# Attention gates of the second macro tile: seven products of quarters in the common order instead of a plain product ahead of the other two groups

## The chip, the cores and the metric

The kernel runs on one core of one Trainium2 chip. The metric is the device time of one execution in microseconds (us); less is better. A core has TensorE (PE, with its weight loads shown as PEld), VectorE (DVE), ScalarE (ACT), GpSimd (POOL) and SyncE (SP), whose queue issues nearly all transfers here. Each engine works through its own instructions in the order in which they were written.

## The reference

One encoder layer over 4096 tokens of width 1024:

```
h = rmsnorm(x, pre_norm_g)
q, k, v, g_a, u_p, g_p = split(h @ w_in)
a = banded_attention(q, k, v, rel_bias, sink) * silu(g_a)   # 8 heads, 2 kv heads, |i-j| <= 128
p = multiscale_pool(u_p, pool_w, pool_scale) * silu(g_p)    # windows 2/4/8/16, mean minus token
x = x + rmsnorm(concat(a, p) @ w_out, post_norm_g)
```

The change touches g_a alone, and the order of the work around it: 512 columns of the input projection, called the attention gates, group QG below.

## The kernel before

The kernel has two halves. The first makes u_p (with pool_w folded into its weights), g_p and g_a, applies the pooling, and stores pooled rows and gates in DRAM (`yp_scr`, `ga_scr`). The second makes q, k and v, the attention and the output projection. The change is in the first half.

**Tiles.** The first half goes over eight macro tiles of 512 tokens, m = 0 to 7; "the second macro tile" is m = 1. The three groups of 512 output columns are QU (u_p), QP (the pool gates) and QG (the attention gates). Every float32 operand is carried as a pair of float16 tiles, a high part and a rest, and a product takes three matmuls: high x high, rest of the weights x high, high x rest of x. The high part is written by ACT (`x_hi`, `t_high`), the rest by DVE (`x_lo`, L303; `t_low`, L526), which reads the high part.

**Products of quarters.** From m = 1 on a group's block of 512 tokens by 512 columns is split in two along tokens, inputs and columns, and is done by seven products of quarters instead of eight (the scheme of Strassen and Winograd). One product (`product`, L990) is 4 x 3 x 2 = 24 matmuls of 128x256. `STEPS` gives the order: A11, A12, S2, S1, S4, S3, A22, where S1 to S4 are sums of quarters of x (`x_sum`, L310, on DVE). In the common order the three groups take turns within each step: QU, QP, QG. After a product ACT copies the PSUM bank (`keep`, L1002), or DVE joins it with a kept one (`join`, L1015); for the gates the SiLU follows on ACT (`gates`, L1024).

**Weights.** `wa` holds for each group seven blocks ("slots") of quarters. Macro tile 0 uses the plain quarters. For the seven products the sums of weight quarters must be formed: `t_sums` (L502, four DVE operations for a pair of column tiles), then `t_high` on ACT (L521) and `t_low` on DVE (L526) for four results of each pair. A group has two pairs: 4 and 5 for QG. Each pair fills one half of the columns of a slot, so a product needs both pairs. Results 3 and 2 go to slots 4 and 2, which the products S2 and S1 read (`t_last`); results 0 and 1 go to slots 5 and 6, for S3 and A22 (`t_first`). Slot 2 holds a plain quarter until then.

**The second macro tile before.** It begins with the attention gates as a plain product: `plain_ga` (L1051), four times 48 matmuls, straight from PSUM through the SiLU. The sums of the QG weights are formed while and after these run. Then QU and QP take their seven products by turns. From m = 2 on all three groups follow the common order.

**What sets the order.** Nothing is scheduled by a tool: `due(t, fn, ...)` notes a time for every step, the plan is sorted by these times, and each engine gets its instructions in that order. The times are only keys of the sort; an instruction runs when its engine reaches it and what it waits for is done. `t1` is the start of macro tile 1 (about 92.4 us in the profile), `PT` = 2.62 a product, `MACRO` = 21 `PT` a macro tile, `T0[m]` the start of tile m.

**Around it.** For macro tile m + 1, during tile m: `x_nat` loads x by rows (`xn`), `x_nat_square` squares them on ACT (L202), `x_scale` makes row scales on POOL, `rs_row` stores them (L268), `rs_spread` reads them back spread over all partitions (`rb`, L272), `y_load` loads x transposed (`ybig`, L282), `y_scale` multiplies (L292, DVE). `pooling(m, j)` is a chain on DVE (L855 to L883) for pooling group j of tile m. During tile 1 the kernel also prepares the weights of v (`wb_tile`; its norm is a small matmul on PE, L427, read by DVE, L133 to L149), and `out_scales` computes small scales on DVE.

Of the kernel before, what the change touches and what calls it, by code (L numbers as in the profile page):

```python
# [71 lines left out]
def hybrid_layer(ctx: ExitStack, tc, io, out):  # L72
# [82 lines left out]
    with ExitStack() as actx:  # L155
# [25 lines left out]
        def due(t, fn, *args):  # L181
            plan.append((t, len(plan), fn, args))
# [852 lines left out]
        def direct_gates(m, q):  # L1035
            silus(m, q, 1, 0, acc_t[m, q, "a"])

        ga_bank = {}

        def plain_ga(m, n, h):  # L1040
            ga_bank[n, h] = acc = (
                psa.tile([P, 2, HALF], F32, name=f"pg{n}{h}", tag="wup", bufs=3) if n
                else gemm.tile([P, 2, HALF], F32, name=f"pg{n}{h}", tag=f"acc{QG}")
            )
            i = 0
            for w in range(2):
                x = couple(m, "XW"[h])[:, w]
                for k in range(HK):
                    for wi, xi in ((0, 0), (1, 0), (0, 1)):
                        for c in range(2):  # L1050
                            nc.tensor.matmul(  # L1051
                                acc[:, c],
                                wa[:, QG, wi, (2 * n + w) * HK + k, c * P : (c + 1) * P],
                                x[:, xi, k, :], start=(i == 0), stop=(i > 3 * 2 * KT - 3),
                                skip_group_check=True,
                            )
                            i += 1

        def plain_gates(m, n, h):
            silus(m, QG, n, h, ga_bank[n, h])  # L1060

        def ga_store(m, n, h):
            s = s_t.pop((m, n, h))
            b0 = m * BPM + 2 * h
# [214 lines left out]
        t_last(5, t1 + 24.0)  # L1279


        def macro_x(m, t, op, s21, s4, s3, ys):

            cast(m, "S4", s4)
            cast(m, "S3", s3)
            if m > 1:
                cast(m, "S2", t + 8.7)
                cast(m, "S1", t + 9.7)
            if m + 1 == NM:
                return  # L1290
# [103 lines left out]

        for m in range(1, NM):
            t0 = T0[m]
            if m == 1:
                quads, z = (QU, QP), t0 + 21.0
            else:
                quads, z = (QU, QP, QG), t0  # L1400
            step = len(quads) * PT

            def op_at(i, z=z, step=step):
                return z + i * step

            if m == 1:
                macro_x(
                    1, t0, op_at, t0 + 15.0, op_at(2) + 0.3, op_at(2) + 1.5,
                    (t0 + 34.0, t0 + 35.2, t0 + 41.0, t0 + 43.6),
                )  # L1410
                x_ahead(3, t0 + 10.0)
            else:
                macro_x(
                    m, t0, op_at, t0 + 11.5, t0 + 17.2, t0 + 19.1,
                    (t0 + 21.0, t0 + 22.2, t0 + 28.5, t0 + 29.7),
                )
                x_ahead(m + 2, t0)
# [1106 lines left out]
```

## Time and profile before

| what | us |
|---|---|
| median of three runs | 1169.52 (1168.46 to 1170.8) |
| span of the profiled execution, first to last instruction | 1163.3 |
| PE busy | 1128.0 (97%) |
| DVE busy | 924.2 (79%) |
| ACT busy | 758.0 (65%) |
| POOL busy | 283.8 (24%) |

The page gives the profiled execution by its span, and no time of its own apart from the three runs; the span is 6.2 below their median, since it leaves out what lies before the first and behind the last instruction. The first half of the kernel reaches to about 490 us. Most of a busy engine's time costs nothing by itself; what counts is what PE waits for, since it is busy nearly all the time. In a timeline a row is a run of like instructions: its start, the time from the start of the first to the end of the last, engine, line, operation, tiles, shapes, how many, and in brackets how long the engine was idle ahead of it and what ended that. In windows a row is a stretch of time with each engine's busy time.

### The profile page before, as it was taken

The page shows a single profiled execution, that of the slowest core. Times are in us where ns is not written, and L with a number is a line of the kernel's source. Part 1 is how long each engine was busy: PE and PEld are TensorE (multiplying, and loading weights), DVE is VectorE, ACT ScalarE, POOL GpSimd, SP SyncE. Part 2 cuts the span into 40 slices and gives each one's busy share as a digit, 9 for nine tenths or more (in the row PEclk, how much of TensorE's full clock was granted, in tenths as well). Part 3 has the DMA queues.
Part 4 walks back from the last instruction along what each step waited for, and adds up shares of the span by engine and source line. Part 5 has one row for each costly group of instructions (what it writes and reads, how often), then busy time and mean ns, then how long its engine had stood idle before and what let it go on. Part 6 is the DMA issues. An engine that isn't in the chain of part 4 may idle for free.

```text
span 1163.3 us, 30484 instructions
## 1 busy us (share of the span) xinstructions
PE 1128.0 (97%) x12528; PEld 833.6 (72%) x12528; DVE 924.2 (79%) x1910; ACT 758.0 (65%) x1696; POOL 283.8 (24%) x270
## 2 busy tenths in 40 slices
PE   5999999999999999999999999999999999999997
PEld 4548888888888888887576676667666666766643
DVE  5788887778878886957887878878778778778896
ACT  5756666676465635166687767777677776777673
POOL 1000000000000000001454444454354444544322
PEclk9999999999999999999999999999999999999999
DMA  9577898696989856989799989899799899899877
GB/s 265 149 237 271 211 259 286 260 310 219 305 244 264 276 198 173 344 285 259 196 191 214 211 213 212 183 235 211 157 228 216 189 219 207 201 222 212 176 187 217
DMA packets 312635, 265.00 MB, mean 228 GB/s; under 512 B 214528, under 2 KB 275584, under 8 KB 303792
## 3 DMA queue, kind: packets, MB, share of 16 engines
q1 hardware_dynamic: 308464, 248.38, 78.1%
q0 software_dynamic: 4032, 14.68, 7.4%
q8 instruction: 98, 1.61, 0.5%
q14 instruction: 41, 0.34, 0.1%
HBM read 132.97 MB, written 79.21 MB: 182 GB/s over the span
## 4 chain that ended last, share of the span: by engine, by line
PE 45%; DVE 3%; DMA 3%; ACT 1%; issue 1%; SPq 0%; DVEq 0%; POOLq 0%; ACTq 0%
PE ms L2017 11%; PE aq_p L1754 9%; PE m L2017 8%; PE s L1532 4%; PE kv L1493 3%; PE kv L1716 3%; PE o L1870 3%; DMA pt_all<-pn 2%; PE z L1989 1%; PE o L1847 1%; DMA xt<-x_scr 1%; DVE pn L1605 1%; DVE p_all L1550 1%; PE ob L1847 1%; PE s L1989 0%
## 5 line engine op out<-in xcount | busy, mean ns | idle before, releaser
L990 PEld LDWEIGHTS <-wa 128*128 128x128 f16 x3360 | 329.7, 98 | 43.5 <-issue 4.8
L990 PE MATMUL ch<-xt,wa 128*128 128x256 f16 x1920 | 214.5, 274 | 2.6 <-ACT cbig L1002 1.7
L1561 ACT ACTIVATE p_all<-p_all,nm 128x384 f32<-128x384 f32 (+1 forms) x256 | 152.4, 596 | 41.3 <-DVE nm L1550 41.3
L1605 DVE SCALAR_TENSOR_TENSOR pn<-p_all,rd,pn 128x384 f16<-128x384 f32 (+1 forms) x256 | 144.5, 624 | 36.9 <-ACT pn L1597 36.1
L2017 PE MATMUL ms<-wo,ys 128*128 128x512 f16 x720 | 165.4, 379 | 2.9 <-DVE ys L1923 0.9
L1597 ACT ACTIVATE pn<-p_all,rd 128x384 f16<-128x384 f32 (+1 forms) x256 | 134.7, 597 | 36.6 <-DVE rd L1583 17.6
L1550 DVE CUSTOM_DVE_ANT_0 p_all<-s,ybig,nsink 128x384 f32<-128x384 f32 (+1 forms) x256 | 155.6, 663 | 1.7 <-PE s L1532 1.7
L2017 PEld LDWEIGHTS <-ys 128*128 128x128 f16 x720 | 68.8, 98 | 83.9 <-issue 2.5
L2017 PE MATMUL m<-wo,y 128*128 128x512 f16 x540 | 124.0, 379 | 1.4 <-DVE mo L2059 1.3
L990 PE MATMUL cl<-xt,wa 128*128 128x256 f16 x960 | 106.7, 273 | 0.8 <-DVE cbig L1015 0.6
L1923 POOL TENSOR_TENSOR y<-yf,y 128x512 f16<-128x512 f32 x29 | 33.5, 1157 | 270.4 <-DMA wo<-w_scr 158.9
L2017 PEld LDWEIGHTS <-y 128*128 128x128 f16 x540 | 51.6, 98 | 62.4 <-issue 2.5
L1754 PEld LDWEIGHTS <-raw 128*128 128x128 f16 x864 | 83.3, 98 | 18.0 <-issue 5.4
L211 POOL TENSOR_SCALAR ssq<-ssq 128x4 f32<-128x4 f32 (+1 forms) x11 | 3.6, 325 | 348.5 <-ACT jk L202 342.7
L1754 PE MATMUL aq_p<-xt,raw 128*128 128x256 f16 x672 | 77.9, 273 | 1.1 <-DVE nm L1550 1.1
L303 DVE TENSOR_TENSOR xt<-ybig,xt 128x1024 f16<-128x1024 f32 x56 | 67.2, 1219 | 13.0 <-ACT xt L298 11.4
L1923 POOL TENSOR_TENSOR ys<-at,ys 128x512 f16<-128x512 f32 x28 | 33.8, 1205 | 147.5 <-ACT ys L1919 123.9
L1532 PE MATMUL s<-k_all,q 64*32 64x288 f16 (+7 forms) x3432 | 63.1, 265 | 1.5 <-ACT k_all L1481 0.9
L1024 ACT ACTIVATE gp<-cbig,cg 128x256 f32<-128x256 f32 x42 | 19.0, 499 | 67.8 <-DVE cbig L1015 64.6
L2054 POOL TENSOR_TENSOR mo<-mo,ybig 128x512 f32<-128x512 f32 x39 | 51.4, 1317 | 44.2 <-ACT jkb L2043 43.9
L298 ACT CAST xt<-ybig 128x1024 f16<-128x1024 f32 x56 | 57.1, 1040 | 4.0 <-PE cl L990 2.1
L1754 PE MATMUL aq_p<-xt,wq_b 128*128 128x256 f16 x504 | 58.6, 273 | 0.0
(211 smaller groups left out, 1948.7 us busy)
## 6 DMA issues: line engine op xcount, KB each, us to landing
x_scr<-xt SPq DMA_DIRECT2D x16, 1024.0 KB
xt<-x_scr SPq DMA_DIRECT2D x16, 1024.0 KB
xn<-in_x SPq DMA_DIRECT2D x28, 512.0 KB
ybig<-in_xT SPq DMA_DIRECT2D x28, 512.0 KB
y_scr<-xt SPq DMA_DIRECT2D x14, 1024.0 KB
xt<-y_scr SPq DMA_DIRECT2D x14, 1024.0 KB
mo<-in_x POOLq DMA_DIRECT2D x28, 512.0 KB, 7.5
out<-mo SPq DMA_DIRECT2D x28, 512.0 KB
```

Of the source, the lines that this page charges most:

```text
L298: nc.scalar.copy(couple(m, c)[:, w, 0], y_view(i))
L303: eng.tensor_tensor(out=o[:, w, 1], in0=y_view(i), in1=o[:, w, 0], op=ALU.subtract)
L990: nc.tensor.matmul(acc[:, c], wa[:, q, wi, slot * HK + k, c * P : (c + 1) * P], x[:, xi, k, :], start=(fresh and n == 0), stop=(n > 3 * 2 ...
L1532: nc.tensor.matmul(s_bank[jj][r0 : r0 + nr, gg, c0:c1], q_t[u, half][a, qi, jj, tl + r0 : tl + r0 + nr], k_all[a, ki, kc : kc + c1 - c0], ...
L1550: nc.vector.tensor_tensor_reduce(out=p_t[b, half][:, hh, :nk], in0=s_t[b, half][jj][:, gg, :nk], in1=bias[:, h, lo : lo + nk], scale=negc[ ...
L1561: nc.scalar.activation(p[:, hh, :nk], p[:, hh, :nk], AF.Exp, bias=nm_t[b, half][:, hh : hh + 1], scale=-1.0, accum_out=den_t[b, half][:, h ...
L1597: nc.scalar.activation(prob_view(b, half)[:, 0, i], p_t[b, half][:, i, :nk], AF.Copy, scale=rd_t[b, half][:, 0, i : i + 1],)
L1605: nc.vector.scalar_tensor_tensor(out=pn4[:, 1, i], in0=p_t[b, half][:, i, :nk], scalar=rd_t[b, half][:, 0, i : i + 1], in1=pn4[:, 0, i], o ...
L1754: nc.tensor.matmul(acc[:, jj], w[:, wi, jj, k, :], x[:, xi, k, :], start=(first and n == 0), stop=(last and n > 3 * 2 * HK - 3), skip_grou ...
L1923: eng.tensor_tensor(out=y[:, :, 1], in0=f(u), in1=y[:, :, 0], op=ALU.subtract)
L2017: nc.tensor.matmul(z_t[u, tag], y[:, k, yi, :], wo[o][:, wi, k, :], start=(n == 0 and acc is None), stop=(n == 3 * HK - 1), skip_group_che ...
L2054: eng.tensor_tensor(out=mo, in0=mo, in1=gpost[:, cs], op=ALU.mult)
```

## The change

The plain product of the attention gates in tile 1 goes. QG takes its seven products in tile 1 by turns with QU and QP, as in the later tiles; tile 1 lasts 21 products, and the later tiles start 2.62 us earlier by the plan. The sums of the QG weights get new times (results 3 and 2 of each pair ahead, 0 and 1 later), and so do the loads of x for tile 2 and 3, the spread of the row scales of tile 2, and the y loads, scalings and casts in tile 1, which follow the later tiles' pattern.

```
-        def plain_ga(m, n, h):
...
-        def plain_gates(m, n, h):
-            silus(m, QG, n, h, ga_bank[n, h])
...
-        x_loads(2, (t1 - 20, t1 - 8), (t1 - 18, t1 + 4), (t1 - 6, t1 + 6), (t1 + 6, t1 + 13))
-        due(t1 + 27.0, rs_spread, 2)
-        for i, n, h in ((0, 0, 0), (1, 1, 0), (2, 0, 1), (3, 1, 1)):
-            due(t1 + 5.24 * i, plain_ga, 1, n, h)
-            due(t1 + 5.24 * i + 5.4, plain_gates, 1, n, h)
-            due(t1 + 5.24 * i + 6.9, ga_store, 1, n, h)
-        t_first(4, t1 + 14.3)
-        t_last(4, t1 + 18.5)
-        t_first(5, t1 + 19.5)
-        t_last(5, t1 + 24.0)
+        x_loads(2, (t1 - 20, t1 - 8), (t1 - 18, t1 - 6.7), (t1 - 6, t1 + 2), (t1 - 5, t1 + 3.3))
+        due(t1 + 14.0, rs_spread, 2)
+        due(t1 + 12.0, t_sums, 4)
+        t_last(4, t1 + 14.9)
+        due(t1 + 16.5, t_sums, 5)
+        t_last(5, t1 + 19.4)
+        for s1, d in ((4, 27.0), (5, 31.0)):
+            for i in (0, 1):
+                due(t1 + d + 1.2 * i, t_high, s1, i)
+                due(t1 + d + 0.75 + 1.2 * i, t_low, s1, i)
...
-        T0 = [0.0, t1] + [t1 + 21.0 + 14 * PT + MACRO * i for i in range(NM - 1)]
+        T0 = [0.0] + [t1 + MACRO * i for i in range(NM)]
...
-            if m == 1:
-                quads, z = (QU, QP), t0 + 21.0
-            else:
-                quads, z = (QU, QP, QG), t0
...
-            if m == 1:
-                macro_x(
-                    1, t0, op_at, t0 + 15.0, op_at(2) + 0.3, op_at(2) + 1.5,
-                    (t0 + 34.0, t0 + 35.2, t0 + 41.0, t0 + 43.6),
-                )
-                x_ahead(3, t0 + 10.0)
...
+            macro_x(
+                m, t0, op_at, t0 + (13.0 if m == 1 else 11.5), t0 + 17.2, t0 + 19.1,
+                (t0 + 21.0, t0 + 22.2, t0 + 28.5, t0 + 29.7),
+            )
+            x_ahead(m + 2, t0)
             for i in range(7):
-                for c, q in enumerate(quads):
+                for c, q in enumerate((QU, QP, QG)):
```

**DVE, early in tile 1.** The place is behind the rests of S2 and S1 of x. `L502` are the sums of weight quarters, `L526` rests of such sums (`wa`), `L1015` joins, `L855` to `L883` pooling, `L303` rests of x (`xt`). Before:

```order
L303 TENSOR_TENSOR xt<-ybig,xt 128x1024 x2
L502 TENSOR_TENSOR cbig<-cbig 128x512 x4
L526 SCALAR_TENSOR_TENSOR wa<-cbig,sc,wa 128x4x128 x3
L502 TENSOR_TENSOR cbig<-raw 128x512
L502 TENSOR_TENSOR cbig<-raw,cbig 128x512
L502 TENSOR_TENSOR raw<-raw 128x512
L502 TENSOR_TENSOR raw<-raw,cbig 128x512
L526 SCALAR_TENSOR_TENSOR wa<-cbig,sc,wa 128x4x128
L526 SCALAR_TENSOR_TENSOR wa<-raw,sc,wa 128x4x128 x2
L526 SCALAR_TENSOR_TENSOR wa<-cbig,sc,wa 128x4x128 x2
L1015 TENSOR_TENSOR u_0_1323<-pb_2_1266,cbig 128x2x256
```

Now, from the second rest of pair 4 (result 2) to the first of pair 5 (result 3), the last that the gates' product S2 needs; ahead of these rows stand the four sums of pair 4, the joins of QU, QP and QG after A12, the pooling of group 0, and pair 4's first rest:

```order
L526 SCALAR_TENSOR_TENSOR wa<-cbig,sc,wa 128x4x128
L502 TENSOR_TENSOR cbig<-raw 128x512
L502 TENSOR_TENSOR cbig<-raw,cbig 128x512
L502 TENSOR_TENSOR raw<-raw 128x512
L502 TENSOR_TENSOR raw<-raw,cbig 128x512
L855 TENSOR_TENSOR ws_1_0_1181<-u_0_632 128x527
L855 TENSOR_TENSOR ws_1_1_1183<-ws_1_0_1181 128x525
L862 TENSOR_TENSOR ws_1_1_1183<-ws_1_1_1183,edge 128x8
L875 SCALAR_TENSOR_TENSOR yt_1_1186<-ws_1_1_1183,u_0_632 128x512
L883 SCALAR_TENSOR_TENSOR yt_1_1186<-yt_1_1186,usc,gp_0_423 128x512
L303 TENSOR_TENSOR xt<-ybig,xt 128x1024
L526 SCALAR_TENSOR_TENSOR wa<-cbig,sc,wa 128x4x128
```

Before, all sums of weights stood ahead of the joins and the pooling; now joins, two pooling groups and the rest of S4 stand among them.

**DVE, late in tile 1.** `L149` ends the norm of v's weights, `L450` to `L701` are small scales, `u_1` is QU's join after S3. Before:

```order
L701 SCALAR_TENSOR_TENSOR rowsc<-rowsc,psc 128x4
L292 TENSOR_TENSOR ybig<-ybig,rb_1292 128x1024
L303 TENSOR_TENSOR xt<-ybig,xt 128x1024
L542 SCALAR_TENSOR_TENSOR raw<-raw,sc 128x1024
L303 TENSOR_TENSOR xt<-ybig,xt 128x1024
L1015 TENSOR_TENSOR u_1_1543<-cl_2_1551,cbig 128x2x256
L855 TENSOR_TENSOR ws_2_0_1608<-u_1_676 128x527
L855 TENSOR_TENSOR ws_2_1_1610<-ws_2_0_1608 128x525
L855 TENSOR_TENSOR ws_2_2_1612<-ws_2_1_1610 128x521
```

Now:

```order
L875 SCALAR_TENSOR_TENSOR yt_2_1493<-ws_2_2_1490,u_1_676 128x512
L883 SCALAR_TENSOR_TENSOR yt_2_1493<-yt_2_1493,usc,gp_1_427 128x512
L450 RECIPROCAL isc<-sc 128x1
L468 TENSOR_REDUCE cga<-sc 128x1
L471 RECIPROCAL cga<-cga 128x1
L472 TENSOR_SCALAR cga<-cga 128x1
L690 TENSOR_TENSOR rowsc<-cga,isc 128x4
L694 TENSOR_TENSOR rowsc<-isc 128x4
L698 TENSOR_SCALAR rowsc<-rowsc 128x4
L701 SCALAR_TENSOR_TENSOR rowsc<-rowsc,psc 128x4
L1015 TENSOR_TENSOR u_1_1411<-cl_2_1448,cbig 128x2x256
L542 SCALAR_TENSOR_TENSOR raw<-raw,sc 128x1024
```

The pooling of group 2 stood behind QU's join and now stands between the norm and that join; on PE the norm's matmul follows QU's product S3, whose result the join reads.

**SP, at the passage from tile 1 to tile 2.** `rs_scr<-ssq` stores the row scales of tile 3, `rb` is their spread, `xn` are x loads of tile 4. Before:

```order
L268 DMA rs_scr<-ssq_1226 128x4x1
L354 DMA raw<-in_w_out 128x1024
L313 DMA x_scr<-xt 128x4096
L272 DMA rb_1729<-rs_scr 128x512
L262 DMA xn_1758<-in_x 128x1024
L262 DMA xn_1764<-in_x 128x1024
```

Now, from the spread on; the store of the row scales stands four transfers of weights and two of gates ahead of it:

```order
L272 DMA rb_1642<-rs_scr 128x512
L889 DMA yp_scr<-yt_3_1608 128x4x128
L313 DMA x_scr<-xt 128x4096
L1042 DMA ga_scr<-sga_0_1_1706 128x2x128 x2
L354 DMA raw<-in_w_out 128x1024
L262 DMA xn_1738<-in_x 128x1024
L262 DMA xn_1746<-in_x 128x1024
```

The x loads now stand behind the last store of gates of tile 1.

More of the change, by code (lines that the diff above doesn't have):

```diff
@@ L1036, in direct_gates @@
             silus(m, q, 1, 0, acc_t[m, q, "a"])
-        ga_bank = {}
-        def plain_ga(m, n, h):
-            ga_bank[n, h] = acc = (
-                psa.tile([P, 2, HALF], F32, name=f"pg{n}{h}", tag="wup", bufs=3) if n
-                else gemm.tile([P, 2, HALF], F32, name=f"pg{n}{h}", tag=f"acc{QG}")
-            )
[L1045 to L1057, printed above, removed]
-        def plain_gates(m, n, h):
-            silus(m, QG, n, h, ga_bank[n, h])
         def ga_store(m, n, h):
@@ L1299, in macro_x @@
             due(op(4) + 7.0, x_store, m + 1, 0)
-            late = 0.1 if m == 1 else 1.9
-            cast(m + 1, "A22", op(6) + late)
-            cast(m + 1, "A21", op(6) + late + (1.1 if m > 1 else 0.5))
+            cast(m + 1, "A22", op(6) + 1.9)
+            cast(m + 1, "A21", op(6) + 3.0)
             due(op(6) + 6.0, x_store, m + 1, 1)
             for i, name in enumerate(("S1", "S3", "S2", "S4")):
-                due(T0[m + 1] - (0.8 if m == 1 else 2.86) + 1.25 * i, x_sum, name)
+                due(T0[m + 1] - 2.86 + 1.25 * i, x_sum, name)
         def x_ahead(m, t, spread=50.0):
@@ L1396, in hybrid_layer, with op_at @@
             t0 = T0[m]
[L1397 to L1417 removed]
+            step = 3 * PT
+            def op_at(i, z=t0, step=step):
+                return z + i * step
+            macro_x(
[3 more added lines that the diff above has]
+            x_ahead(m + 2, t0)
             for i in range(7):
[L1419 removed]
+                for c, q in enumerate((QU, QP, QG)):
                     t = op_at(i) + c * PT
```

## The prediction, written before the run

> **What bounds the kernel now.** I read the page first (PE 97% busy), then the stages of the first half by windows, then the timelines of PE and DVE at the second macro tile, then the waits of the third. Times are us from the start of the span; "rest" is the low f16 half of a pair, written on DVE after ACT has written the high half.
>
> PE, timeline: the four plain products of the gates, the first products of the other two groups, the end of macro tile 1, two waits in macro tile 2, the start of 3.
>
> ```profile
> 92.56 21.12 PE L1051 MATMUL pg<-xt,wa 128*128 128x256 f16 x192
> 113.52 5.40 PE L990 MATMUL ch<-xt,wa 128*128 128x256 f16 x48
> 118.76 5.40 PE L990 MATMUL pb<-xt,wa 128*128 128x256 f16 x48
> 148.09 2.78 PE L990 MATMUL cl<-xt,wa 128*128 128x256 f16 x24 [0.20 <-DVE cbig L1015]
> 150.96 8.02 PE L990 MATMUL ch<-xt,wa 128*128 128x256 f16 x72
> 175.44 0.38 PE L427 MATMUL n<-wsq,ones 128*128 128x2 f32 x2 [0.74 <-ACT wj L423]
> 176.85 17.55 PE L990 MATMUL ch<-xt,wa 128*128 128x256 f16 x144 [1.03 <-ACT cbig L1002]
> 209.96 8.02 PE L990 MATMUL ch<-xt,wa 128*128 128x256 f16 x72
> ```
>
> Two products of 24 matmuls take 118.76 - 113.52 = 5.24, so one takes 2.62 and a matmul 0.109. PE never waits from 92.56 to 148; it is the bound there. Macro tile 1 lasts 150.96 - 92.56 = 58.4, macro tile 2 lasts 59.0. The windows of tiles 2 and 3 (columns: length, PE, PEld, DVE, ACT, POOL busy, clock, DMA) show what is odd about tile 2:
>
> ```profile
> 150.90:209.90 59.00, 57.17 (x506) 50.35 (x506) 45.84 (x61) 38.38 (x77) 1.81 (x2) 0.97 0.84 243
> 209.90:265.80 55.90, 55.47 (x511) 49.62 (x509) 45.26 (x58) 38.65 (x77) 1.79 (x2) 1.00 0.85 297
> ```
>
> The same products take 3.1 less in tile 3. Tile 2 waits 1.8 for ACT (rows above), and then the granted clock falls:
>
> ```profile
> 176.85:178.00 1.15, 1.15 (x9) 0.90 (x9) 0.95 (x2) 1.15 (x2) 0.00 (x0) 0.76 1.11 318
> 178.00:180.00 2.00, 2.00 (x11) 1.45 (x10) 2.00 (x2) 1.84 (x4) 0.00 (x0) 0.50 0.94 301
> 180.00:181.50 1.50, 1.50 (x12) 1.19 (x11) 1.47 (x4) 0.00 (x0) 0.00 (x0) 0.72 0.97 323
> ```
>
> That is 0.24 x 1.15 + 0.50 x 2.0 + 0.28 x 1.5 = 1.7 of lost clock after about 2 us in which PE hardly worked.
>
> **The change part by part.**
>
> *A, fewer matmuls.* 192 plain matmuls go, 7 x 24 = 168 come: 24 x 0.109 = 2.6 less on PE, all of it on the path. The waits at the old end of tile 1 (0.20, and 150.96 - 148.09 - 2.62 = 0.25) go with the old order. A = -3.1. Tile 1 without waits would take 21 x 2.62 = 55.0.
>
> *B, the sums of the gate weights.* This decides. Until now the 21 us of plain products, which read stored quarters, were the time in which DVE formed the sums. Now the gates' third product needs the rests of both pairs of sums. It is due after eight products: 92.56 + 8 x 2.62 = 113.5. DVE stands here:
>
> ```profile
> 95.09 0.75 DVE L526 SCALAR_TENSOR_TENSOR wa<-cbig,sc,wa 128x512 f16<-128x512 f32 x1 [1.86 <-ACT wa L521]
> ...
> 102.94 2.35 DVE L303 TENSOR_TENSOR xt<-ybig,xt 128x1024 f16<-128x1024 f32 x2
> 105.21 2.62 DVE L502 TENSOR_TENSOR cbig<-cbig 128x512 f32<-128x512 f32 x4
> ...
> 112.01 0.69 DVE L502 TENSOR_TENSOR cbig<-raw 128x512 f32<-128x512 f32 x1
> ...
> 114.54 0.74 DVE L526 SCALAR_TENSOR_TENSOR wa<-cbig,sc,wa 128x512 f16<-128x512 f32 x1
> ...
> 124.17 0.69 DVE L1015 TENSOR_TENSOR u<-pb,cbig 128x512 f32<-128x512 f32 x1 [3.72 <-PE pb L990]
> ...
> 125.38 0.70 DVE L855 TENSOR_TENSOR ws<-u 128x527 f32<-128x527 f32 x1
> ...
> 127.70 1.22 DVE L303 TENSOR_TENSOR xt<-ybig,xt 128x1024 f16<-128x1024 f32 x1
> ...
> 131.20 0.70 DVE L855 TENSOR_TENSOR ws<-u 128x527 f32<-128x527 f32 x1
> ...
> 134.27 1.22 DVE L292 TENSOR_TENSOR ybig<-ybig,rb 128x1024 f32<-128x1024 f32 x1
> ```
>
> DVE works without a gap from 95.09 to 107.8, on work that the change leaves alone up to the rest of S2 at 102.94. From there the new order puts ahead of the last rest that the third product needs: three rests of x (2.27 for two, so 1.14 each: 3.4), three joins (125.38 - 124.17 = 1.21 for two: 1.8), two groups of four sums (114.54 - 112.01 = 2.5 each: 5.1), pooling of group 0 (127.70 - 125.38 = 2.3) and of group 1 (134.27 - 131.20 = 3.1), and three rests of sums at 0.7 (2.2). That is 17.9: it ends at 120.8. ACT writes the high halves meanwhile; each of its jobs is short beside what DVE has in front, so I charge nothing for it; if it came late, B would grow. PE, in order, has nothing else: B = 120.9 - 113.5 = +7.4. By summed durations instead of starts, the chain would be some 0.9 longer; with a join or pooling group less in front, 2 to 3 shorter: 5 to 8.5.
>
> *C, the clock after B.* Such a wait is not in the trace. Nearest rows: 1.7 lost after the 2 us above, and nothing after one wait of 1.3 (clock column 1.00):
>
> ```profile
> 574.55 2.75 PE L2017 MATMUL m<-wo,y 128*128 128x512 f16 x12 [1.30 <-DVE mo L2059]
> 574.00:576.00 2.00, 1.45 (x7) 0.68 (x7) 2.00 (x6) 1.47 (x5) 0.86 (x2) 1.00 0.86 164
> ```
>
> A wait of 7 is nearer to the first: C = +1.7, between 0.9 and twice that, 3.4. [...]
>
> *D, DVE at the end of tile 1.* The weight norm's matmul keeps its due time, which now lies behind the sixth product of the u group. DVE waits for it in order; behind it stand five small operations, pooling of group 2, eight small ones, and only then the join that the u group's last product needs.
>
> ```profile
> 135.41 0.15 DVE L133 TENSOR_REDUCE m<-n 128x1 f32<-128x1 f32 x1
> ...
> 136.34 0.16 DVE L450 RECIPROCAL isc<-sc 128x1 f32<-128x1 f32 x1
> ...
> 136.86 1.21 DVE L292 TENSOR_TENSOR ybig<-ybig,rb 128x1024 f32<-128x1024 f32 x1
> ...
> 140.62 1.28 DVE L542 SCALAR_TENSOR_TENSOR raw<-raw,sc 128x1024 f16<-128x1024 f32 x1
> ...
> 143.56 0.69 DVE L855 TENSOR_TENSOR ws<-u 128x527 f32<-128x527 f32 x1
> ...
> 147.36 0.68 DVE L1015 TENSOR_TENSOR cbig<-cl,cbig 128x512 f32<-128x512 f32 x1
> ...
> 153.69 0.70 DVE L855 TENSOR_TENSOR ws<-u 128x527 f32<-128x527 f32 x1
> ...
> 158.23 2.48 DVE L310 TENSOR_TENSOR ybig<-ybig 128x1024 f32<-128x1024 f32 x2
> ```
>
> From the end X of that product: norm matmuls and signal 0.4, five small 0.9, pooling 147.36 - 143.56 = 3.8, eight small 1.0 (four take 136.86 - 136.34 = 0.5), join 0.6: X + 6.7. PE has two products, X + 5.4: a wait of 1.3. After it DVE still has L542 with 1.3, two joins 1.2, pooling of group 3 (158.23 - 153.69 = 4.5), join 0.6, two rests 2.3, one x sum 1.2 (two at 158.23 take 2.48), the pool gates' last join 0.6: X + 18.4. PE would open that bank again at X + 6.7 + 4 x 2.62 = X + 17.2: 1.2 more, and 0.5 for the gates' join behind two more sums. D = +3.0, between 0 (if DVE's queue is shorter) and 4.
>
> *E, macro tile 2.* Its 1.8 of waits and 1.7 of clock come from one queue: SP holds the spread of row scales until the rows have landed, and the x loads behind it.
>
> ```profile
> 147.94 0.95 SPq L268 DMA_DIRECT2D rs_scr<-ssq  x1
> ...
> 161.78 0.32 SPq L272 DMA_DIRECT2D rb<-rs_scr  x1
> 162.15 1.64 SPq L262 DMA_DIRECT2D xn<-in_x  x2
> 168.21 1.06 ACT L202 ACTIVATE jk<-xn 128x1024 bf16<-128x1024 f32 x1 [4.17 <-DMA xn<-in_x]
> 199.71 0.50 SPq L268 DMA_DIRECT2D rs_scr<-ssq  x1
> ...
> 209.36 0.33 SPq L272 DMA_DIRECT2D rb<-rs_scr  x1
> ```
>
> Rows to spread took 13.8 there, 9.7 one tile later. With the change the rows of tile 3 leave SP behind the store of pooling group 2, near X + 6, which is about 9 ahead of tile 2 (before: 150.96 - 147.94 = 3), so the spread goes out at the tile's start + 1 to 5, and the x loads, behind the last gate store, at + 8 to 10.5 instead of + 11.2. ACT then waits up to 3 instead of 4.2, and PE enters with the slack that D's waits leave. I take tile 3's length: E = -3.1, between -3.8 and 0.
>
> *At no cost.* Three more copies on ACT lie beside products, 0.6 each:
>
> ```profile
> L1002 ACT COPY cbig<-ch 128x512 f32<-128x512 f32 x6 | 3.5, 580 | 4.2 <-PE ch L990 4.2
> ```
>
> Two x loads of tile 2 and their squares move ahead, so tile 2's row scales leave SP near 102. Their spread moves past the loads of tile 3's x and of a weight; by the landing times above it may hold SP and the weight load behind it until 112 to 116. DVE reaches the first use only behind B's chain, after 121; without that cover DVE would wait up to 3 at that place.
>
> Sum: -3.1 + 7.4 + 1.7 + 3.0 - 3.1 = +5.9. The profiled span, 1163.3, would become 1169.2; the median of the runs stands 6.2 above the span (what lies before and behind it), so 1169.5 becomes 1175.4.
>
> **Rivals.**
> - *The sums come in time* (faster). If DVE's chain ended by 113.5, B and C vanish: -3.1 + 3.0 - 3.1 = -3.2, 1166.3. For: the due times put the last rest at 112.5. Against: 17.9 of work from 102.94. It turns at B + C = 3.2, so a chain under some 13.
> - *Tile 2 keeps its wait*: E = 0, 1178.5. For: the gate store ahead of the x loads. Against: the earlier rows.
> - *No jam at the end*: D = 0, 1172.4. For: before, the old join there cost 0.2. Against: the in-order queue behind the norm.
> [...]
>
> **How the numbers follow.** Forecast 50%, in time 6%, tile 2 keeps its wait 16%, no jam 16%, long low clock 12%. Within 0.2% (2.3 us, about what this kernel's runs tell from no change) means 1167.2 to 1171.8: it needs B near 5 with D = 0, or the sums nearly in time, and gets 7%; faster 7%; slower 86%. The range 1171 to 1180 reaches from no jam with a shorter B to a kept wait with a long low clock.
>
> **What would show it.** PE: no L1051, a wait of about 7 at the gates' third product with the gate weights (DVE, L526) as releaser, then a clock near 0.5 for some 3 us; waits of 1 to 1.5 on L1015 at the seventh u product and the next tile's first pool gate product; tile 2 without its drop in clock. It is wrong if DVE reaches that rest by 113.5, or if tile 2's loads come late again.

## The result and the profile after

| | median us | ratio to the kernel before, 95% interval |
|---|---|---|
| before, same chip | 1169.57 (1168.46 to 1170.8) | |
| changed | 1177.03 (1176.42 to 1177.6) | 1.0065 [1.0051, 1.0079] |
| changed, run again on another chip (before there 1168.54) | 1178.47 (1174.94 to 1179.71) | 1.0088 [1.0069, 1.0106] |

The change costs 7.5 us, where 5.9 was forecast; 1177.03 lies inside the range of 1171 to 1180. The profiled execution of the changed kernel took 1177.48 with a span of 1175.7, so only 1.8 lie outside the span. That corrects the text above: of the 6.2 between the span of before and its median, about 4.4 are not work outside the span, but an execution that was quicker than the three shown (wherever both times are on record, 1.7 to 2.0 lie outside). The two spans therefore differ by 12.4, more than the medians do, and the spans alone would overstate the change.

Where the time went is seen by tiles. A tile's length is the time from its first product (QU's, but the plain gates' in tile 1 of the kernel before) to that of the next tile, read off PE's timeline; the windows of tiles 1 to 3 of the changed kernel (columns as before: length, PE, PEld, DVE, ACT, POOL busy, clock, DMA) are:

```profile
93.33:158.20 64.87, 57.33 (x507) 50.15 (x506) 51.04 (x79) 37.51 (x69) 3.94 (x4) 0.95 0.78 187
158.20:216.74 58.54, 55.89 (x508) 49.52 (x506) 43.96 (x56) 38.91 (x79) 2.15 (x2) 1.00 0.82 278
216.74:274.53 57.79, 55.45 (x510) 49.60 (x508) 45.23 (x58) 38.65 (x77) 1.91 (x2) 1.00 0.84 287
```

The first window holds 58.40 before, so tile 1 is 6.5 longer, tile 2 0.5 shorter (59.00), tile 3 1.9 longer (55.90): 7.9 in all, close to the 7.5 of the medians. The other 4.5 of the 12.4 are 0.8 ahead of tile 1, 1.7 in tiles 4 to 6 and 2.0 behind them. Over the twelve traces of this study these last two parts go from 166.0 to 169.3 and from 729.8 to 733.0; what lies behind tile 6 shows no relation to what was edited. Tile 5 does: it lasts 55.16 in the four traces with x loaded early (below) and in the kernel before, 55.23 in e7, and 55.70 to 57.73 in the other six, 56.23 in the changed kernel. So up to 1.1 of the 1.7 may belong to the change; one trace of the kernel before can't show it.

PE's timeline of tile 1 and the start of tile 2, changed kernel:

```profile
109.05 5.51 PE L990 MATMUL ch<-xt,wa 128*128 128x256 f16 x49
117.42 0.39 PE L990 MATMUL ch<-xt,wa 128*128 128x256 f16 x2 [2.85 <-ACT wa L521]
121.50 19.84 PE L990 MATMUL ch<-xt,wa 128*128 128x256 f16 x165 [3.69 <-DVE wa L526]
...
150.35 8.02 PE L990 MATMUL cl<-xt,wa 128*128 128x256 f16 x72 [1.00 <-DVE u L1015]
158.20 2.78 PE L990 MATMUL ch<-xt,wa 128*128 128x256 f16 x24
161.88 2.78 PE L990 MATMUL ch<-xt,wa 128*128 128x256 f16 x24 [0.89 <-DVE cbig L1015]
164.87 1.36 PE L990 MATMUL ch<-xt,wa 128*128 128x256 f16 x11 [0.21 <-DVE cbig L1015]
```

PE does 48 matmuls of QU and QP and one of the gates' third product, then waits 2.85 for a high half on ACT, does two, and waits 3.69 for the last rest on DVE: 6.5. At the end of tile 1 and the start of tile 2 stand three waits with joins (L1015) as releasers: 2.1. DVE's timeline shows both causes, its chain ahead of the rest and the weight norm ahead of the join:

```profile
103.71 1.22 DVE L303 TENSOR_TENSOR xt<-ybig,xt 128x1024 f16<-128x1024 f32 x1
...
120.70 0.75 DVE L526 SCALAR_TENSOR_TENSOR wa<-cbig,sc,wa 128x512 f16<-128x512 f32 x1
...
144.12 0.16 DVE L133 TENSOR_REDUCE m<-n 128x1 f32<-128x1 f32 x1 [4.95 <-PE n L427]
...
149.61 0.68 DVE L1015 TENSOR_TENSOR u<-cl,cbig 128x512 f32<-128x512 f32 x1
```

From 103.71 to 121.45 DVE needs 17.7 for the chain that was added up to 17.9. At the end it first stands idle for 4.95, since the norm's matmul has not run on PE, and only then does pooling and the join. The clock after the long wait, in windows of 2 us:

```profile
121.50:123.50 2.00, 2.00 (x10) 1.44 (x11) 2.00 (x3) 0.00 (x0) 0.00 (x0) 0.50 1.10 341
123.50:125.50 2.00, 2.00 (x14) 1.51 (x13) 2.00 (x2) 0.00 (x0) 0.00 (x0) 0.64 1.15 349
```

It lost 0.50 x 2 + 0.36 x 2 = 1.7. The last piece is tiles 2 and 3, PE first, then ACT at the x loads, then SP's queue around the passage from tile 1 to tile 2, and what SP waited for there between 160 and 170 (in all, times, longest):

```profile
183.89 0.38 PE L427 MATMUL n<-wsq,ones 128*128 128x2 f32 x2 [0.52 <-ACT wj L423]
185.30 15.88 PE L990 MATMUL ch<-xt,wa 128*128 128x256 f16 x144 [1.03 <-ACT cbig L1002]
...
242.82 5.40 PE L990 MATMUL ch<-xt,wa 128*128 128x256 f16 x48 [2.33 <-ACT cbig L1002]
```

```profile
176.62 1.06 ACT L202 ACTIVATE jk<-xn 128x1024 bf16<-128x1024 f32 x1 [1.44 <-DMA xn<-in_x]
...
234.10 1.06 ACT L202 ACTIVATE jk<-xn 128x1024 bf16<-128x1024 f32 x1 [2.14 <-DMA xn<-in_x]
```

```profile
149.31 0.46 SPq L268 DMA_DIRECT2D rs_scr<-ssq  x1
...
159.84 0.33 SPq L272 DMA_DIRECT2D rb<-rs_scr  x1
...
166.26 1.57 SPq L1042 DMA_DIRECT2D ga_scr<-sga  x2
...
169.19 1.77 SPq L262 DMA_DIRECT2D xn<-in_x  x2
```

```profile
SPq L1042 <- DMA raw<-in_w_b: 3.0, 2, 2.2
```

The spread left 1.6 behind the start of tile 2, as forecast, but the x loads left only at + 11.0, no sooner than before (+ 11.2). Two things held SP's queue ahead of them. The gate stores need the last SiLU of tile 1, which ended at 165.8; and by SP's waits they and their neighbours were let go one by one as transfers of weights landed that had left at 150 to 152 (2.7 at the store of x, 3.0 at the two gate stores, of which 1.8 lie ahead of the SiLU's end, and 0.9 at the weight load behind them). Tile 2 still waits 1.55, this time without a fall of the clock. In tile 3 there is a wait that the kernel before hardly had: ACT waits 2.14 for x (0.24 before), PE 2.33 for the copy behind it. PE at that place before:

```profile
234.13 5.40 PE L990 MATMUL ch<-xt,wa 128*128 128x256 f16 x48 [0.43 <-ACT cbig L1002]
```

### The profile page after: what moved, and what is told of

Same layout as the page of the kernel before. It is cut to its first block, busy times and chain, and to the rows that moved or that the text cites. A ratio compares the mean times of both kernels' runs of the same rounds, so it can differ in the third digit from the quotient of the medians.

```text
span 1175.7 us, 30451 instructions
## 1 busy us (share of the span) xinstructions
PE 1126.4 (96%) x12504; PEld 831.6 (71%) x12504; DVE 924.9 (79%) x1913; ACT 759.2 (65%) x1699; POOL 287.0 (24%) x270
## 4 chain that ended last, share of the span: by engine, by line
PE 61%; DVE 14%; DMA 9%; issue 7%; ACT 3%; SPq 1%; POOL 0%; DVEq 0%; POOLq 0%; ACTq 0%
PE ms L1981 11%; PE aq_p L1718 10%; PE m L1981 8%; PE ch L990 7%; PE s L1496 4%; PE cl L990 4%; DVE ws L855 3%; PE kv L1457 3%; PE kv L1680 3%; PE a L940 3%; PE o L1834 3%; DVE xt L303 2%; DMA pt_all<-pn 2%; DMA xn<-in_x 2%; PE pb L990 2%
## 5 line engine op out<-in xcount | busy, mean ns | idle before, releaser
L990 PEld LDWEIGHTS <-wa 128*128 128x128 f16 x3528 | 345.9, 98 | 59.7 <-issue 11.9
L990 PE MATMUL ch<-xt,wa 128*128 128x256 f16 x2016 | 225.5, 274 | 12.7 <-DVE wa L526 3.7
L990 PE MATMUL cl<-xt,wa 128*128 128x256 f16 x1008 | 112.4, 273 | 3.9 <-DVE u L1015 2.9
L303 DVE TENSOR_TENSOR xt<-ybig,xt 128x1024 f16<-128x1024 f32 x56 | 67.3, 1219 | 19.6 <-ACT xt L298 13.3
L1496 PEld LDWEIGHTS <-q 64*32 64x32 f16 (+1 forms) x3432 | 42.9, 91 | 21.3 <-issue 16.6
```

What stands on the lines that cost most here:

```text
L303: eng.tensor_tensor(out=o[:, w, 1], in0=y_view(i), in1=o[:, w, 0], op=ALU.subtract)
L990: nc.tensor.matmul(acc[:, c], wa[:, q, wi, slot * HK + k, c * P : (c + 1) * P], x[:, xi, k, :], start=(fresh and n == 0), stop=(n > 3 * 2 ...
L1496: nc.tensor.matmul(s_bank[jj][r0 : r0 + nr, gg, c0:c1], q_t[u, half][a, qi, jj, tl + r0 : tl + r0 + nr], k_all[a, ki, kc : kc + c1 - c0], ...
```

## The experiments

Each kernel but one starts from the changed one. They ran on three chips, on which executions spread more than in the first table (before from 1164.5 to 1172.2), so ratios to the kernel before, run beside each kernel, are compared, and the tiles by their lengths in the traces:

| kernel | ratio [95%] | tile 1 | tile 2 | tile 3 | sum |
|---|---|---|---|---|---|
| before | 1 | 58.40 | 59.00 | 55.89 | 173.3 |
| changed | 1.0065 [1.0051, 1.0079] | 64.87 | 58.54 | 57.79 | 181.2 |
| changed, again (e8) | 1.0088 [1.0069, 1.0106] | 64.54 | 60.29 | 57.39 | 182.2 |
| e1: pooling behind the rests | 1.0038 [1.0024, 1.0052] | 61.22 | 58.50 | 58.00 | 177.7 |
| e2: all sums first | 1.0055 [1.0036, 1.0074] | 59.78 | 58.66 | 59.86 | 178.3 |
| e3: pooling 2 ahead of the norm | 1.0043 [1.0028, 1.0059] | 63.47 | 56.01 | 57.56 | 177.0 |
| e4: x loads early | 1.0023 [1.0012, 1.0034] | 66.05 | 57.26 | 55.55 | 178.9 |
| e7: sums first, pooling late | 1.0020 [1.0007, 1.0033] | 57.75 | 58.86 | 57.64 | 174.3 |
| e10: sums first, pooling in the idle gaps | 1.0011 [1.0001, 1.0021] | 56.50 | 58.88 | 57.73 | 173.1 |
| e5: e7, e3 and e4 together | 0.9970 [0.9956, 0.9985] | 59.56 | 55.16 | 55.57 | 170.3 |
| e9: e10, e3 and e4 together | 0.9943 [0.9930, 0.9955] | 55.60 | 56.74 | 55.57 | 167.9 |
| e6: kernel before, x loads early | 0.9943 [0.9926, 0.9961] | 59.01 | 55.16 | 55.55 | 169.7 |

**e1, the pooling out of the chain.** Groups 0 and 1 are pooled after the rests instead of among them.

```
+ d = 11.9 if m == 1 else 0.0
- pooling(m - 1, 2 * n, t + (1.0 if n else 3.5))
+ pooling(m - 1, 2 * n, t + (1.0 if n else 3.5 + d))
- pooling(m - 1, 2 * n + 1, t + (3.9 if n else 6.0))
+ pooling(m - 1, 2 * n + 1, t + (3.9 if n else 6.0 + d))
```

> The changed kernel, with pooling of groups 0 and 1 in tile 1 moved behind the rests of the gates' weight sums on DVE, and nothing else. Theory (DVE's queue ahead of the last rest of the sums is the wait): 5.4 us of that queue go; then ACT's high halves come in between (its gates wait for a join first), so the rest ends near 117.8 instead of 121.4 and the wait at the gates' third product falls from 6.5 us to about 3.5; 1173 to 1174 if the clock still falls, 1172 if not. Rival (the extra copies and joins, or the moved transfers, make the loss): the wait stays, 1177.

PE's timeline at the gates' third product:

```profile
116.25 0.39 PE L990 MATMUL ch<-xt,wa 128*128 128x256 f16 x2 [2.26 <-ACT wa L521]
117.27 19.85 PE L990 MATMUL ch<-xt,wa 128*128 128x256 f16 x165 [0.62 <-DVE wa L526]
```

The wait fell from 6.5 to 2.9, by 3.6 of the 5.4 us of pooling moved; tile 1 is 3.65 shorter. The rest of the 5.4 is a wait of DVE's own for ACT's high half, which pooling had covered. The 165 matmuls behind it took as long as in the changed kernel (19.84), so the clock fell again: a shorter wait, the same 1.7. Times the first chip's 1169.57, the ratio is 1174.0. That is the theory.

**e2, the sums first.** Both pairs' sums and the eight needed parts directly behind the rests of S2 and S1 of x.

```
- t_last(4, t1 + 14.9)
- due(t1 + 16.5, t_sums, 5)
- t_last(5, t1 + 19.4)
+ due(t1 + 12.1, t_sums, 5)
+ for i, d in ((3, 12.5), (2, 13.9)):
+     for c in (0, 1):
+         due(t1 + d + 0.1 * c, t_high, 4 + c, i)
+         due(t1 + d + 0.7 + 0.1 * c, t_low, 4 + c, i)
```

> The changed kernel, with the sums of the second pair right behind those of the first and the high halves and rests of both right behind them, ahead of joins and pooling; the same instructions in another order. Theory: the last rest that the third product needs is done by about 113.7, before PE comes to it (114.3), so wait (6.5) and low clock (1.7) both go: 1168.5 to 1169. Rival (DVE has too much work in this tile whatever the order): the wait comes back a little later, at the joins or the rests of x, and the time stays above 1173.

The wait at the third product is gone, but PE waits one product later, for ACT. Three timelines, PE (and a row from tile 3), ACT and DVE:

```profile
119.86 15.88 PE L990 MATMUL ch<-xt,wa 128*128 128x256 f16 x144 [3.28 <-ACT cbig L1002]
...
237.91 6.90 PE L990 MATMUL ch<-xt,wa 128*128 128x256 f16 x48 [2.90 <-ACT cbig L1002]
```

```profile
117.49 0.91 ACT L1024 ACTIVATE sga<-cbig,cg 128x256 f32<-128x256 f32 x2 [3.64 <-issue]
118.30 1.03 ACT L298 CAST xt<-ybig 128x1024 f16<-128x1024 f32 x1
119.24 0.57 ACT L1002 COPY cbig<-ch 128x512 f32<-128x512 f32 x1
```

```profile
116.72 0.68 DVE L1015 TENSOR_TENSOR cbig<-pb,cbig 128x512 f32<-128x512 f32 x1
```

The gates' join of A12 now comes behind sums, pooling and rests on DVE (116.72); ACT, in order, holds its SiLU and behind it the cast of S4 and the copy that frees QU's bank; PE wants that bank at 116.6. So 1168.5 to 1169 was missed (the ratio times 1169.57 is 1176.0): 6.5 of wait became 3.3, and in tile 3 the clock fell at the wait (48 matmuls in 6.90, 5.40 in the changed kernel). The theory named the right place, and the rival was right that DVE's queue, not this one rest, sets the time there.

**e3, the norm's place.** Pooling group 2 moves ahead of the weight norm on DVE.

```
- pooling(0, 2, t + 6.0)
+ pooling(0, 2, t + 3.0)
```

> The changed kernel, with pooling of group 2 in tile 1 ahead of the norm of v's weights on DVE, where DVE sat idle for 5 us waiting for the norm. Theory: the waits of 1.0, 0.9 and 0.2 at the end of tile 1 go, 1175 (-2.1). Rival (DVE is late there because of the long wait earlier): the waits stay, 1177.

All three waits of D are gone; the last five products of tile 1 are one row, and the first three of tile 2 another:

```profile
143.21 13.26 PE L990 MATMUL cl<-xt,wa 128*128 128x256 f16 x120
156.31 8.02 PE L990 MATMUL ch<-xt,wa 128*128 128x256 f16 x72
```

Tile 1 is 1.4 and tile 2 is 2.5 shorter, 3.9 where 2.1 was expected; by the ratio 2.6 are gained. Of the 2.5, 1.4 are D, counted from start to start of the matmuls (a row's end is modelled, and the marked waits, 1.1 here, leave out some 0.17 each); the rest is less waiting in the middle of tile 2 (0.72 marked instead of 1.55).

**e4, the x loads early.** From tile 4's x on, the first two x loads leave SP ahead of the spread.

```
- x_loads(m, (t + 3, t + 11.8), (t + 4, t + 12.9), (t + 24, ...
+ a = (-6.0, -5.9) if m > 3 else (3, 4)
+ x_loads(m, (t + a[0], t + 11.8), (t + a[1], t + 12.9), (t + 24, ...
```

> The changed kernel, with the first two x loads of each tile from tile 2 on issued ahead of the spread of row scales on SP, 9 us earlier. Theory (SP, held by the spread until its rows have landed, keeps the x loads back, and ACT waits for them ahead of the copies that PE needs): the waits of 0.5 and 1.0 in tile 2 and of 2.3 in tile 3 go, 1173. Rival (the transfers are short of bandwidth, and the loads only push others back): 1177, with other waits.

SP's queue, and PE in tiles 2 and 3:

```profile
150.07 0.46 SPq L268 DMA_DIRECT2D rs_scr<-ssq  x1
...
152.82 1.52 SPq L262 DMA_DIRECT2D xn<-in_x  x2
...
165.28 0.33 SPq L272 DMA_DIRECT2D rb<-rs_scr  x1
```

```profile
184.79 15.88 PE L990 MATMUL ch<-xt,wa 128*128 128x256 f16 x144 [0.54 <-ACT cbig L1002]
...
231.95 13.30 PE L990 MATMUL ch<-xt,wa 128*128 128x256 f16 x118
```

The loads leave 6 us ahead of tile 2 instead of 11 behind its start; ACT no longer waits for them, tile 3's wait of 2.33 is gone and tile 2's 1.55 is down to 0.54. Tiles 2 and 3 are 3.5 shorter. By the ratio 4.9 us are gained, though tile 1 of the profiled execution lost 1.2 more than the changed kernel's, through the clock (last section).

**e7, B and C alone.** e2's edit with the pooling of e1, and the cast of S4 behind the copy (t0 + 18.7 instead of t0 + 17.2).

> The changed kernel with the weight sums first, pooling groups 0 and 1 behind their rests and the cast of S4 behind the copy, but the norm's order and the x loads as in the change. Theory (B and C come from the rests standing behind joins and pooling on DVE): the 6.5 us of waits at the gates' third product fall to under 1, the clock does not fall, tile 1 lasts about 57.3 (55.2 and D's 2.1) instead of 64.9; tiles 2 and 3 as in the changed kernel, with their waits of 1.5 and 2.3; tiles 1 to 3 about 173.5, as much as before: ratio 0.999 to 1.001. Rival (DVE's queue as a whole): a wait of 2 or more comes up at a later product in tile 1, tile 1 lasts 60 or more, ratio over 1.002.

There is no wait and no fall of the clock from 93.5 to 141, so B and C are gone. But D has grown. DVE and PE:

```profile
118.20 2.36 DVE L303 TENSOR_TENSOR xt<-ybig,xt 128x1024 f16<-128x1024 f32 x2 [2.44 <-ACT xt L298]
122.32 2.36 DVE L292 TENSOR_TENSOR ybig<-ybig,rb 128x1024 f32<-128x1024 f32 x2 [1.76 <-DMA rb<-rs_scr]
```

```profile
143.43 8.02 PE L990 MATMUL cl<-xt,wa 128*128 128x256 f16 x72 [2.27 <-DVE u L1015]
```

DVE now stands idle for 4.2, in waits that the pooling had covered, and the pooling, still to be done behind them, makes the join before the last product of QU late: 2.27 instead of 1.00. A wait of over 2 at a later product is what the rival expected; a tile 1 of 57.75 is near the theory's 57.3 and far from the rival's 60. The ratio, 1.002, lies between the two, and its interval reaches into both.

**e5, all edits.** e7 with e3's and e4's.

> The changed kernel with all four edits together: both pairs' weight sums and their needed rests formed ahead of anything else behind the rests of x, pooling groups 0 and 1 behind those rests, the cast of S4 of x behind ACT's copy of QU's third product (so that the gates' late SiLU does not hold that copy), pooling group 2 ahead of the weight norm, and the first two x loads ahead of the spread on SP. Theory (the losses B, C, D and E are separate and each has the cause named): no wait over 0.6 us on PE in tiles 1 to 3 and no fall of the clock; tile 1 lasts 55.2 to 56, tile 2 56, tile 3 55.6, so tiles 1 to 3 take about 167 against 173.3 in the kernel before: 6.3 less, 0.9946 of its time. Rival (DVE's queue as a whole is the limit early in tile 1): removing one wait there makes another of 2 to 3 us with its clock loss, tiles 1 to 3 about 171 to 172, 0.998 to 0.999.

Tiles 2 and 3 came out as the theory had them (55.16 and 55.57). Tile 1 did not: the same idle of 4.2 on DVE as in e7, a wait of 2.41 at QU's last product, and here the clock fell behind it (72 matmuls in 9.69, not 8.02). The ratio lies between the two theories.

**e9, pooling where DVE stood idle.** Only the times of the pooling differ from e5.

```
- d = 11.9 if m == 1 else 0.0
+ a, b = (2.9, 4.0) if m == 1 else (0.0, 0.0)
- pooling(m - 1, 2 * n, t + (1.0 if n else 3.5 + d))
+ pooling(m - 1, 2 * n, t + (1.0 if n else 3.5 + a))
- pooling(m - 1, 2 * n + 1, t + (3.9 if n else 6.0 + d))
+ pooling(m - 1, 2 * n + 1, t + (3.9 if n else 6.0 + b))
```

> e5_all with one thing changed: pooling group 0 stands right behind the join of the gates and group 1 behind the rest of S3, so that they lie where DVE stood idle in e5_all (2.44 us for ACT's high half of S4 and 1.77 for the spread of row scales), no longer behind these waits. Theory (the 2.4 us of PE's wait left in e5_all is that idle time, given back later by the late pooling): DVE's idle at both places goes, the join that the last product of QU needs ends near 138.9 instead of 143.2 and ahead of 140.9, where PE needs it; no wait over 0.5 and no fall of the clock in tile 1, which lasts 55.2 to 55.6 instead of 59.6; 0.993 to 0.994 of the kernel before. Rival (DVE is simply full in tile 1): the idle goes but the wait stays at 1.5 to 2.5, tile 1 57.5 to 59.5, ratio 0.996 to 0.997.

PE's timeline of the end of tile 1 and the start of tile 2:

```profile
108.64 23.91 PE L990 MATMUL ch<-xt,wa 128*128 128x256 f16 x216
...
135.14 13.54 PE L990 MATMUL cl<-xt,wa 128*128 128x256 f16 x120
148.52 2.78 PE L990 MATMUL ch<-xt,wa 128*128 128x256 f16 x24
152.19 2.78 PE L990 MATMUL ch<-xt,wa 128*128 128x256 f16 x24 [0.89 <-DVE cbig L1015]
```

Tile 1 lasts 55.60 without a wait that the timeline marks: DVE could do all its work in time, in another order. The two idle gaps are closed, and a new one of 1.76 (for a y load) costs nothing. The ratio, 0.9943, is the theory's. Not foreseen: two of D's waits, 0.89 and 0.21 at the start of tile 2, are back, 1.1.

**e10, the same without e3's and e4's edits.**

> The changed kernel with the sums first, the cast of S4 behind the copy and the pooling of groups 0 and 1 placed as in e9_fill, and nothing else: the norm's order and the x loads stay as in the change. It leaves D and E alone and shows what B and C cost. Theory: tile 1 lasts 55.2 to 55.6 (changed kernel 64.9), the 0.9 and 0.2 at the start of tile 2 stay, tile 2 near 58.5, tile 3 near 57.7; tiles 1 to 3 about 171.6 and the whole 0.9995 to 1.0005 of the kernel before. Rival (DVE is full): a wait of 1.5 to 2.5 at the last product of QU as in e7_sums_pool, ratio 1.002.

PE and DVE at the end of tile 1:

```profile
141.65 8.02 PE L990 MATMUL cl<-xt,wa 128*128 128x256 f16 x72 [1.02 <-DVE u L1015]
```

```profile
135.40 0.16 DVE L133 TENSOR_REDUCE m<-n 128x1 f32<-128x1 f32 x1 [2.19 <-PE n L427]
```

Tile 1 is 56.50, of which 1.02 is the first wait of D, to the hundredth as in the changed kernel (1.00), although PE reaches that product 8.7 us earlier: DVE waits for the norm whenever it comes, and pooling and join follow it. The expectation overlooked this 1.0; the ratio is 1.0011 instead of 1.000. Without B and C the change is at most 0.2% slower than before, and the sum of tiles 1 to 3 is the same (173.1).

**e6, the kernel before with the x loads early** (e4's edit there).

> The kernel before, with one edit: from tile 4's x on, the first two x loads leave SP 6 us ahead of the tile's start instead of 3 us behind it, ahead of the spread of row scales. Theory (the loss in tile 2 of the kernel before comes from SP holding the x loads behind the spread): the waits of 0.74 and 1.03 in tile 2 shrink below 0.6 in sum, the clock stays at 1.00, tile 2 lasts 56 to 57 instead of 59.0; 2 to 3 us less in all, ratio 0.9975 to 0.998. Rival (the waits come from ACT's own queue or the clock fell by itself): tile 2 stays at 58.5 to 59, ratio 1.000.

Windows of tile 2 and tile 3:

```profile
151.73:206.89 55.16, 55.16 (x507) 49.46 (x506) 45.93 (x60) 38.24 (x77) 1.81 (x2) 1.00 1.02 260
206.89:262.44 55.55, 55.46 (x510) 49.60 (x508) 45.32 (x58) 38.54 (x77) 1.79 (x2) 1.00 0.94 304
```

Tile 2 waits nowhere and its clock stays at 1.00: 3.8 shorter. The ratio gained more, 0.9943, some 6.7 us. Its profiled execution is only 4.4 ahead of that of before at the start of tile 7, and that execution of before, 1163.3 + 1.8, was itself some 3.4 quicker than the median of before here. The mean clocks of the executions on record (0.998 for the kernel before, 0.999 here, of 1168 us) account for about 1 of the missing 2 to 3. Whether the usual execution of before loses more at these loads than the profiled one stays open, since it left no trace.

**e8, the changed kernel again.**

> The changed kernel itself, on this chip, so that the three others can be compared with it and the parts of its loss with each other. Both theories: ratio 1.0065 within 0.0015, tile 1 near 64.9, tiles 1 to 3 about 181, with the waits of 2.8 and 3.7 at the gates' third product. If tiles 1 to 3 come out the same but the whole differs from 1.0065 by more, the rest lies in the second half and is spread between executions.

Tiles 1 to 3 took 182.2; the ratio is a little above what was expected, with an interval that reaches into it. One thing differs, and it matters for E; the same place as the row at 185.30 above:

```profile
184.62 17.55 PE L990 MATMUL ch<-xt,wa 128*128 128x256 f16 x144 [1.03 <-ACT cbig L1002]
```

The wait is the same to the hundredth; the 144 matmuls behind it take 1.67 longer.

**The best versions.** e9 and e6 are both 0.57% faster than the kernel before, each on its own chip. Both load x early, so what is left between them is the change with its other losses repaired: in the traces tiles 1 to 3 of e9 are 1.8 shorter, but the ratios and the medians (1161.17 and 1160.86, with runs from 1160.6 to 1161.3 and from 1159.0 to 1163.5) don't tell them apart. That the change itself gains anything is not shown.

## Why the prediction was right, and where it was not

| term | forecast | measured | how |
|---|---|---|---|
| A, fewer matmuls | -3.1 | -2.75 | tile 1 less waits and clock, 64.87 - 6.5 - 1.7 - 1.0 = 55.65, against 58.40 |
| B, the gates' third product | +7.4 | +6.5 | the two waits of 2.85 and 3.69 |
| C, the clock | +1.7 | +1.7 | windows behind 121.50 |
| D, end of tile 1 | +3.0 | +2.1 | 1.00 + 0.89 + 0.21 |
| E, tiles 2 and 3 | -3.1 | +0.3 | 58.54 - 1.1 - 59.0 = -1.6 and 57.79 - 55.89 = +1.9 |
| sum | +5.9 | +7.9 | medians +7.5 |

The waits are taken as the timeline marks them, each some 0.17 short (161.88 - 158.20 - 2.62 = 1.06 beside a marked 0.89). Counted from start to start of the matmuls, A is -3.3, B +6.9, D +2.6 and E 0.0; the sum stays.

- **B and C** carried the sign, and were right in cause and size. The chain on DVE came out as added up, from starts of rows in the kernel before. The last rest ended at 121.45, forecast 120.8, while tile 1 started 0.8 later: 17.7 against 17.9. From PE's due time, 93.33 + 8 x 2.62 = 114.3, to 121.50 are 7.2; three matmuls were done in between, which leaves 6.9, and the timeline marks 6.5 as waits. Charging nothing for ACT held for the sum, not in the order of waits: the first 2.85 is booked on ACT, whose high half of pair 5 starts at 116.64, right behind DVE's sums of that pair (they end at 116.58) and behind a cast of its own. e1 shows the pooling's share, e7 and e10 that without the chain both terms vanish.
- **D** had the right three places and the right cause (e3 takes all three away), forecast 1.3 + 1.2 + 0.5, measured 1.00 + 0.89 + 0.21. The terms that were mis-sized are the lengths on both sides, a little each: counted from the end of QU's product, 141.18 + 2.62 = 143.80, the join ended at + 6.5 (forecast 6.7) and PE was there at + 5.55 (5.4).
- **E is the step that failed**: "the x loads, behind the last gate store, at + 8 to 10.5", and "I take tile 3's length". The spread was freed as forecast, but the loads left at + 11.0: the gate stores ahead of them left only at 166.26, behind the last SiLU and behind landings of transfers of weights, which the forecast had not counted. PE's two waits stayed (1.55 of 1.77). So the rival "tile 2 keeps its wait" described tile 2, and by the prediction's own sign ("if tile 2's loads come late again") this part was wrong. That tile 2 came out 0.5 shorter all the same was luck: the clock did not fall in this execution and did in e8, where E is 60.29 - 1.1 - 59.0 and 57.39 - 55.89, together +1.7 (last section). Tile 3's wait was in no term: x left SP 6.5 behind the start of tile 3 (223.22 - 216.74), ACT waited 2.14 for it. e4 and e6 show that the place of these loads on SP is the cause of tile 3's wait and of most of tile 2's.
- **At no cost**: "without that cover DVE would wait up to 3" was right, and seen when the cover was taken away: 2.69 in e1, 1.76 in e7. The spread itself left SP at 116.85, just past the forecast's 116.
- **The base**: the sum was put on the median of 1169.5, which was right; that the 6.2 between it and the span lies outside the span was wrong (1.8 does).
- Of the rivals, "the sums come in time" would have needed a chain under 13; it was 17.7. "No jam" was wrong. The long low clock, given 12%, a loss of 3.4 in place of C's 1.7, is a term that no run shows: in the changed kernel's trace 1.7 were lost, since the clock was at half for 6.8 us but PE waited in the first half of it, and the most was 2.9, in e4. The forecast of 1175.4 lay only 1.6 under the result by luck: E had 3.4 too much gain and A 0.35, and B and D, each forecast 0.9 too high by the marked waits, made up about half of that.

## What to carry to other kernels

When work loses the phase that covered it, add up, in the in-order engine that does it, everything that the new order puts ahead of the operation that is needed, from starts in the old trace; that sum was right to 0.2 us. Moving late operations about moves the wait to whatever then stands behind (e2, e7), until the displaced work fills the engine's idle gaps (e9): look for these first. And look at the kernel before for a stall that the change is credited with curing: a single line there (e6) gave as much as the change with all its repairs, that line among them.

## What the runs showed of the hardware

**The length of a wait alone does not tell whether it cost clock in these traces.** Of waits of PE in these traces, listed by length: 1.64 (e8, tile 2), 1.77 (kernel before, tile 2), 2.41 (e5), 2.88 in two parts (e1) and 2.90 (e2, tile 3) cost 1.5 to 1.7 us of clock; 1.55 (changed kernel, tile 2), 1.87 and 1.90 (e7 and e10, tile 2), 2.27 (e7), 2.33 (changed kernel, tile 3), 2.55 (e1, tile 3) and 3.28 (e2, tile 1) cost none.

The granted clock, as recorded in the two traces of the first comparison: in the kernel before it rises at 17.01, falls at 177.44, rises at 180.85 and falls at 1160.48, the last three 47, 48 and 335 steps of 3.413 us behind the first; in the changed kernel it does so at 19.11, 118.09, 124.92 and 1172.81, 29, 31 and 338 such steps behind the first. Counted off in these steps, a wait lies in one of them or is shared by two. With the small matmuls of the norm (L427) counted as idle time, PE was idle for 3.41 - 1.64 + 0.38 = 2.15 us of the step before the fall in the kernel before (174.03 to 177.44) and for 3.02 of the one in the changed kernel (114.68 to 118.09). The waits of 2.41 (e5) and 2.27 (e7) stand at the same place; for each, the step that holds most of the wait and the next (length, PE, PEld, DVE, ACT, POOL busy, clock, DMA), e5 first:

```profile
141.23:144.64 3.41, 1.34 (x13) 1.20 (x13) 3.24 (x14) 1.15 (x1) 0.00 (x0) 1.00 2.15 174
144.64:148.05 3.41, 3.41 (x19) 2.43 (x17) 3.31 (x6) 2.98 (x6) 0.00 (x0) 0.50 0.29 18
```

```profile
139.68:143.09 3.41, 1.47 (x14) 1.18 (x12) 3.24 (x13) 0.00 (x0) 0.00 (x0) 1.00 0.61 213
143.09:146.50 3.41, 3.07 (x29) 2.75 (x29) 3.38 (x6) 1.30 (x4) 0.00 (x0) 1.00 1.51 100
```

PE is idle for 3.41 - 1.34 = 2.07 in e5's step, and the clock is at half in the next; in e7's it is idle for 1.94, and the rest of the wait, 0.34, lies in the next step, which runs at the full clock. The 3.28 of e2, in steps counted back from the fall at 237.62 in its tile 3, are shared as 1.56 and 1.72. In tile 2 of the changed kernel the first trace has 3.41 - 1.86 + 0.38 = 1.93 of idle in one step (182.94 to 186.35) and no fall behind it, e8 has 2.02 (181.83 to 185.24) and a fall. No limit is shown by this: the clock of e1 fell behind a step with some 1.9 of idle.

The clock was at half for one step, 3.4 us, after the waits that cost 1.5 to 1.7, for two in the changed kernel after its 6.5 of waits (118.09 to 124.92), and in e4 until 126.89, where PE resumed at 121.09. Two rows from there:

```profile
121.09:123.09 2.00, 2.00 (x10) 1.45 (x11) 2.00 (x3) 0.00 (x0) 0.00 (x0) 0.50 1.11 342
...
125.09:127.09 2.00, 2.00 (x13) 1.46 (x11) 0.01 (x1) 0.58 (x1) 0.00 (x0) 0.55 1.06 368
```

With the row between them 0.50 x 2 + 0.50 x 2 + 0.45 x 2 = 2.9 were lost while PE worked. The 165 matmuls behind this wait took 19.84, 19.60 (e3), 19.50 (e8) and 21.00 (e4), where 165 x 0.109 = 18.0 and 0.16 for the end of the last are the full clock: so C is 1.3 to 1.7 in three of these traces and 2.9 in e4. Of the waits listed, none under 1.64 cost clock; between 1.64 and 3.28 some did and some did not; the 6.3 to 6.5 of the changed kernel, e3, e4 and e8 did in all four.

**A store of 2 KB of row scales held its spread for 10 to 15 us in these traces.** By SP's waits the landing let the spread go 13.8 and 9.7 behind the store in the kernel before, 14.7 (tile 1), 10.5 (the passage to tile 2) and 10.0 (to tile 3) in the changed kernel. Other transfers left in between as long as they stood ahead of the spread in the queue; in front of the spread itself SP stood still for 10.8 in the kernel before and for 4.5 in the changed one at the passage to tile 2. In e4 the spread left 15.2 behind the store (150.07 to 165.28), and the x loads, now ahead of it in the queue, at 152.82. In the queues shown nothing behind the spread left before it; what only needs SP, and not the rows, belongs ahead of it.
